# Moving the start addresses of the tiles that the matrix engine reads: a two-layer trunk in fp32r

## The chip, the cores and the metric

The kernel runs on one core of one Trainium2 chip. The time is device time in microseconds of that core, a median of several executions; one further execution was recorded by the hardware profiler, and every row of the profile below comes from it. Where a time in nanoseconds is given for "one matmul", the text says whether it is the duration of its record or the distance from its start to the start of the next one.

## The reference, cut to what matters

One sequence of 256 tokens with 2048 channels passes through two layers. Layer 0 mixes by a gated causal convolution beside a sparse attention of 16 heads, layer 1 by a causal pooling; each layer then has an MLP with a squared ReLU, 2048 to 8192 to 2048. All arithmetic is float32.

```
for layer in range(DEPTH):
    x = x + even_mixer(...) if layer % 2 == 0 else x + odd_mixer(...)
    x = x + mlp(x, mlp_norm[layer], w_mlp_in[layer], w_mlp_out[layer])
return rmsnorm(x, final_norm)

def mlp(x, g, w1, w2):
    h = rmsnorm(x, g) @ w1
    h = jnp.square(jax.nn.relu(h))
    return h @ w2
```

Nearly all the work is products of 256 tokens with weight matrices: the input and output projections of layer 0, and the two matrices of each MLP.

## The kernel before, in words

**Three products for one.** A float32 product is done as three products in the one-pass format fp32r. A weight unit of 128 partitions x 2048 floats is loaded into a tile `wraw`; ScalarE rounds it into `whi`, and VectorE writes the rest into `wlo` (class `Weights`, method `pieces`). The activations are split in the same way: `xT` holds, for each block of 128 channels, 256 columns of rounded values and 256 columns of rests. Then hi x hi, hi x rest and rest x hi are accumulated in PSUM. Every matmul goes through `mm` (line 194), so line 194 stands for all of them in the profile, and the names of the tiles tell them apart.

**Narrow and wide matmuls.** For a matmul the engine first loads 128 columns of one operand as its weights and then streams the other operand through. There are two shapes:

- narrow, in `unit_cols` (layer 0's projections) and in `unit_wide` and `first_hidden` (first matrix of the MLPs): 128 columns of `whi` or `wlo` are loaded, 256 columns of `xT` are streamed. In `keys_values` the roles are turned for the values: 128 columns of `xT` are loaded and 256 columns of `whi` or `wlo` streamed (shown as acc<-whi,xT).
- wide, in `product` (second matrix of the MLPs), in `by_token` (output projection, pooling) and in the end of `run_mlp`: 128 columns of an activation tile are loaded (the tiles `f11`, `f12`, `f22`, `s1` to `s4`, or `yo`, `yc`, `xT`) and 512 columns of `whi` or `wlo` are streamed.

In the profile the streamed operand and the loaded one stand behind the arrow (acc<-xT,whi is narrow, acc<-whi,f wide). Within a tile all these slices begin at multiples of 512 bytes from the tile's start, so each operand has the start of its tile, modulo 256 bytes, for all its matmuls.

**Order.** The program of each engine is written in order; the weight units come in the order of `_uses`, three raw tiles ahead (`RAW_BUFS`) and three split ones (`W_BUFS`). Between the products of the second matrix (12 wide matmuls each) stand units of the first matrix for the next chunk (48 narrow matmuls each).

**Where tiles lie.** A pool is a stretch of each partition, and its tiles follow one another in the order of their first use, each rounded up to 32 bytes. From the low end lie `const` (small tiles), `wpool` (three `wraw`, three `whi`, three `wlo`, 8192 bytes each) and `act` (the slot "xr", which holds `xraw`, `ctile` and the residual `x` in turn, then four slots of `xT`, 8192 bytes each, which `yo` and the residual's parts `xt` use too). A pool on the right side ends at the top of the partition, so a larger pool begins lower: `mix` in layer 0's mixer, `mlp` afterwards. Tiles named `fill` are never read or written; they only move what follows. Counted in bytes, the program before has these starts:

| tile | start | start modulo 256 |
|---|---|---|
| `wraw`, `whi`, `wlo` | 24640, 49216, 73792 (first of each three) | 64 |
| slot "xr" | 98368 | 64 |
| `xT`, `yo` | 115712 (first of four) | 0 |
| `kk2`, `klo` (keys, streamed) | 193024, 201216 | 0 |
| `yc`, `wg` | 155136, 163328 (the two slots that they share) | 0 |
| `q` (loaded for the scores) | 219008 | 128 |
| `f11` and the other forms | 193280 and on | 0 |
| `pm` (loaded for the pooling means) | 150176 | 160 |

Of the kernel before, what the change touches and what calls it, by code (L numbers as in the profile page):

```python
# [27 lines left out]
F32 = mybir.dt.float32  # L28
# [6 lines left out]
P = 128  # L35
# [6 lines left out]
HEADS = 16  # L42
# [137 lines left out]
def trunk(ctx: ExitStack, tc: tile.TileContext, a: dict, out: bass.AP, dump: dict | None = None):  # L180
# [3 lines left out]
    const = ctx.enter_context(tc.tile_pool(name="const", bufs=1, side="left"))  # L184
    wpool = ctx.enter_context(tc.tile_pool(name="wpool", bufs=1, side="left"))
    act = ctx.enter_context(tc.tile_pool(name="act", bufs=1, side="left"))
# [25 lines left out]
    nc.gpsimd.dma_start(ident, a["ident"])  # L212

    identr = const.tile([P, P], F32R, name="identr")
    const.tile([P, 32], F32, name="fill")
    neg_half = const.tile([P, 2], F32, name="neg_half")
    vector.memset(neg_half, -0.5)

# [59 lines left out]
    with ExitStack() as mx:  # L278
        mix = mx.enter_context(tc.tile_pool(name="mix", bufs=1, side="right", reuse_waits="tile"))
# [3 lines left out]
        def acc1(n=256, dt=F32):  # L283
            return ps.tile([P, 512], dt, tag="acc", bufs=8, name="acc")[:, 0:n]
# [86 lines left out]
        def unit_cols(*accs, done=lambda: None):  # L371

            ws = [W.next(16) for _ in accs]
            for u in range(4):
                X = xT[u]
                for acc, w in zip(accs, ws):
                    for k in range(4):
                        kk_ = 4 * u + k
                        st, sp = kk_ == 0, kk_ == 15
                        if len(w) == 1:  # L380
                            mm(acc, w[0][:, kk_], x32[kk_ // 8][:, kk_ % 8], start=st, stop=sp)
                        else:
                            hi, lo = w
                            mm(acc, hi[:, kk_], X[:, k, 0:256], start=st, stop=False)
                            mm(acc, hi[:, kk_], X[:, k, 256:512], start=False, stop=False)
                            mm(acc, lo[:, kk_], X[:, k, 0:256], start=False, stop=sp)
                if u == 3:
                    done()
                beside(u)
# [33 lines left out]
        def glu(g, late_g, a, late_a, out):  # L423
            sg = mix.tile([P, 256], F32, tag="row", bufs=4, name="sg")
            if late_g:
                vector.tensor_mul(sg, g, rbc)
            nc.scalar.activation(sg, sg if late_g else g, AF.Sigmoid)
            if late_a:
                vector.tensor_mul(sg, sg, rbc)
            vector.tensor_mul(out, a, sg)  # L430
# [4 lines left out]
        for ct in range(1, 8):  # L435
            g, a_ = acc1(), acc1()
            late = [W.used + i < PLAIN for i in range(2)]
            unit_cols(g)
            if ct == 1:

                ctile = act.tile([P, 8 * 286 + 8 * 256], F32, tag="xr", bufs=1, name="ctile")
                cin = ctile[:, 0:8 * 286].rearrange("p (c t) -> p c t", c=8)
                cacc = ctile[:, 8 * 286:].rearrange("p (c t) -> p c t", c=8)
                nc.gpsimd.memset(cin[:, :, 0:30], 0.0)
                glu(g0, True, a0, True, cin[:, 0, 30:286])
            unit_cols(a_)
            glu(g, late[0], a_, late[1], cin[:, ct, 30:286])
            conv_ready = ct + 1
# [4 lines left out]
        for i in range(2):  # L453
            t = mix.tile([P, KT, P], F32, tag="q8", bufs=2, name="w1")
# [5 lines left out]
        for i in range(2):  # L460
            t = mix.tile([P, 512], F32, tag="tt", bufs=3, name="wgl")[:, 0:384]
# [117 lines left out]
        keys_values(1)  # L579
        assert not steps  # L580

        gates = mix.tile([P, 2, HEADS, 3], F32, name="gates")
        pg = acc1()[0:112]
        for k in range(KT):
            X, w = xT[k // 4], wg[0][:, k]
# [7 lines left out]
        def gates_1():  # L593
# [5 lines left out]
            vector.tensor_add(g, g, pgt[:, :, 0:48])  # L599
            nc.scalar.activation(g, g, AF.Sigmoid)  # L600

        masks = const.tile([P, P + 33], F32, name="masks")
        nc.gpsimd.dma_start(masks, a["masks"])
        cmaskr = const.tile([P, P], F32R, name="cmaskr")
# [383 lines left out]

        banks_for("ps3")

        mix.tile([P, 24], F32, name="fill")
        x = act.tile([P, 2, D], F32, tag="xr", bufs=1, name="x")
        turns = []

# [21 lines left out]
    mlp = ctx.enter_context(tc.tile_pool(name="mlp", bufs=1, side="right", reuse_waits="tile"))  # L1016
# [240 lines left out]


    pm = mlp.tile([P, 3, 4, P], F32R, name="pm")

    def load_pm(i):
        pmf = mlp.tile([P, 4, P], F32, tag="s", bufs=3, name="pmf")
        nc.scalar.dma_start(pmf.rearrange("p g t -> p (g t)"), a["pm"][:, i * 512:(i + 1) * 512])
        return lambda: nc.scalar.activation(pm[:, i], pmf, AF.Copy)
# [233 lines left out]
```

## Time and profile before

| | |
|---|---|
| median of 3 runs | 1753.16 us (1749.74 to 1760.92) |
| the profiled execution: its own time | 1751.68 us |
| its span, first to last instruction | 1749.9 us |
| TensorE busy | 1737.2 us (99%), 11726 matmuls |
| VectorE busy | 1488.3 us (85%) |
| ScalarE busy | 1083.4 us (62%) |
| mean DMA rate | 229 GB/s |
| granted TensorE clock | 0.998 |

A record of a matmul lasts longer than the distance to the next one, because matmuls are pipelined: a row with 11726 matmuls of some 280 to 390 ns each adds up to less than their product. The rate at which the engine really goes is read from a stretch of time: its length divided by the number of matmuls that began in it. The answers by stretches count the records that lie in a stretch even in part; of the narrow and wide records two that began earlier still run at its start, so two are taken off the count.

### The profile page before, as it was taken

To read this page: it belongs to the slowest core of one execution; us is meant where nothing else is said; L and a number is where in the kernel's file an instruction comes from. 1 tells how busy PE (TensorE), PEld (TensorE's weight loads), DVE (VectorE), ACT (ScalarE), POOL (GpSimd) and SP (SyncE) were. 2 spreads that over 40 slices of the span, in tenths; PEclk is the share of its full clock that TensorE was granted. 3 is DMA by queue.
4 is the path that set the end of the run, shared out by engine and by line. 5 is a ranking of instruction groups with operands and counts; after the bars stand their busy time and mean duration, and the time that the engine had idled before them with its cause. 6 is when DMAs were issued, how large, how long until landed. Compare 5 with 4: busy or idle time off the path is not lost.

```text
span 1749.9 us, 28680 instructions
## 1 busy us (share of the span) xinstructions
PE 1737.2 (99%) x11726; PEld 1593.1 (91%) x11726; DVE 1488.3 (85%) x1851; ACT 1083.4 (62%) x1626; POOL 61.8 (4%) x82
## 2 busy tenths in 40 slices
PE   9999999999999999999999999999999999999997
PEld 7999998889999999999999989999999999999986
DVE  6998998766888888898889869688888889898985
ACT  4445666556666666665666655766665666666663
POOL 2000000000000000000000000000000000000000
PEclk9999999999999999999999999999999999999999
DMA  7654323546878787878778764687877787878873
GB/s 279 232 207 145 122 94 125 207 177 217 261 252 267 240 255 242 282 245 290 241 241 256 228 232 147 228 269 248 256 246 257 243 290 244 268 240 251 257 232 127
DMA packets 58948, 399.89 MB, mean 229 GB/s; under 512 B 6672, under 2 KB 7456, under 8 KB 11712
## 3 DMA queue, kind: packets, MB, share of 16 engines
q1 hardware_dynamic: 47904, 331.90, 49.3%
q0 software_dynamic: 8608, 61.49, 18.8%
q10 hardware_dynamic: 2304, 4.67, 0.8%
q8 instruction: 92, 1.51, 0.3%
q14 instruction: 40, 0.33, 0.1%
HBM read 395.93 MB, written 2.10 MB: 227 GB/s over the span
## 4 chain that ended last, share of the span: by engine, by line
PE 99%; issue 0%; DMA 0%; DVE 0%; ACT 0%; POOLq 0%; POOL 0%; ACTq 0%; DVEq 0%
PE acc L194 94%; PE S L194 2%; PE PV L194 1%; PE T L234 1%; PE acc L234 1%; PE T L194 0%; DMA xraw<-in_xT 0%; DVE x L78 0%; POOLq L1494 0%; POOL rs L1374 0%; DVE q L78 0%; ACT sq L1369 0%; DVE nb L78 0%; DVE wlo L78 0%; ACT yo L237 0%
## 5 line engine op out<-in xcount | busy, mean ns | idle before, releaser
L194 PE MATMUL acc<-xT,whi 128*128 128x256 f32 x4992 | 867.8, 278 | 0.0
L194 PEld LDWEIGHTS acc<-xT,whi 128*128 128x128 f32 x4992 | 763.6, 188 | 10.0
L78 DVE TENSOR_TENSOR wlo<-wraw,whi 128x1024 fp32r<-128x1024 f32 (+1 forms) x552 | 605.0, 1125 | 146.3 <-ACT whi L147 145.3
L194 PE MATMUL acc<-xT,wlo 128*128 128x256 f32 x2496 | 691.7, 277 | 0.0
L147 ACT ACTIVATE whi<-wraw 128x1024 fp32r<-128x1024 f32 (+1 forms) x552 | 515.3, 974 | 100.8 <-PE acc L194 85.0
L194 PEld LDWEIGHTS acc<-xT,wlo 128*128 128x128 f32 x2496 | 469.0, 188 | 0.0
L78 DVE TENSOR_TENSOR wlo<-z,whi 128x1024 fp32r<-128x1024 f32 x224 | 266.7, 1217 | 60.7 <-ACT whi L147 59.8
L194 PE MATMUL acc<-whi,s 128*128 128x512 f32 x960 | 315.9, 391 | 0.0
L147 ACT ACTIVATE whi<-z 128x1024 fp32r<-128x1024 f32 x224 | 230.5, 1054 | 93.9 <-DVE z L78 76.1
L194 PE MATMUL acc<-whi,f 128*128 128x512 f32 x864 | 282.3, 392 | 0.0
L194 PEld LDWEIGHTS acc<-whi,s 128*128 128x128 f32 x960 | 180.3, 188 | 35.8
L1045 ACT ACTIVATE t<-acc 128x256 f32<-128x256 f32 x128 | 48.8, 381 | 243.3 <-PE acc L194 242.8
L194 PEld LDWEIGHTS acc<-whi,f 128*128 128x128 f32 x864 | 162.3, 188 | 31.8
L194 PE MATMUL acc<-wlo,s 128*128 128x512 f32 x480 | 188.1, 392 | 0.0
L194 PE MATMUL acc<-wlo,f 128*128 128x512 f32 x432 | 169.3, 392 | 0.0
L194 PEld LDWEIGHTS acc<-wlo,s 128*128 128x128 f32 x480 | 90.1, 188 | 18.6
L78 DVE SCALAR_TENSOR_TENSOR ctile<-ctile,cw 128x256 f32<-128x256 f32 x240 | 102.1, 480 | 0.1
L194 PEld LDWEIGHTS acc<-wlo,f 128*128 128x128 f32 x432 | 81.1, 188 | 16.3
L78 DVE SCALAR_TENSOR_TENSOR x<-acc,r,x 128x512 f32<-128x512 f32 x110 | 81.2, 744 | 7.8 <-PE acc L194 7.8
L1090 ACT ACTIVATE s<-s 128x512 fp32r<-128x512 f32 x56 | 35.4, 632 | 62.5 <-DVE s L78 62.5
L78 DVE TENSOR_TENSOR z<-z,b 128x1024 f32<-128x1024 f32 x56 | 65.9, 1218 | 0.0
L78 DVE TENSOR_TENSOR z<-z,wraw 128x1024 f32<-128x1024 f32 x56 | 65.8, 1214 | 0.0
(213 smaller groups left out, 1360.3 us busy)
## 6 DMA issues: line engine op xcount, KB each, us to landing
wraw<-in_ws SPq DMA_DIRECT2D x254, 1024.0 KB, 6.4
z<-in_ws SPq DMA_DIRECT2D x28, 1024.0 KB, 7.2
b<-in_ws SPq DMA_DIRECT2D x28, 1024.0 KB, 4.8
b<-in_ws POOLq DMA_DIRECT2D x28, 1024.0 KB, 8.9
z<-in_ws POOLq DMA_DIRECT2D x28, 1024.0 KB, 8.3
w<-in_cmp_w POOLq DMA_DIRECT2D x2, 1024.0 KB, 6.8
xraw<-in_xT SPq DMA_DIRECT2D x3, 512.0 KB, 6.1
wraw<-in_ws SPq DMA_DIRECT2D x6, 256.0 KB, 6.2
```

Of the source, the lines that this page charges most:

```text
L78: return fn(*args, **kw)
L147: nc.scalar.activation(hi[:, c], raw[:, c], AF.Copy)
L194: nc.tensor.matmul(out, w, x, **kw)
L234: nc.tensor.transpose(out, src, ident[0:n, 0:n])
L1045: nc.scalar.activation(out, acc, AF.Relu)
L1090: nc.scalar.activation(F[tag][:, :, 0:P], src(), AF.Copy)
```

## The change

Only sizes and fillers change; no instruction is added, removed or moved.

```diff
@@ trunk, pool const @@
     identr = const.tile([P, P], F32R, name="identr")
-    const.tile([P, 32], F32, name="fill")
+    const.tile([P, 8], F32, name="fill")
@@ slot "xr" of pool act @@
-                ctile = act.tile([P, 8 * 286 + 8 * 256], F32, tag="xr", bufs=1, name="ctile")
+                ctile = act.tile([P, 8 * 286 + 8 * 256], F32, tag="xr", bufs=1, name="ctile",
+                                 padded_shape=[P, 8 * 286 + 8 * 256 + 32])
                 cin = ctile[:, 0:8 * 286].rearrange("p (c t) -> p c t", c=8)
-                cacc = ctile[:, 8 * 286:].rearrange("p (c t) -> p c t", c=8)
+                cacc = ctile[:, 8 * 286:8 * 286 + 8 * 256].rearrange("p (c t) -> p c t", c=8)
@@ pool mix @@
-        gates = mix.tile([P, 2, HEADS, 3], F32, name="gates")
+        gates = mix.tile([P, 128], F32, name="gates")[:, 0:96].rearrange("p (t h b) -> p t h b", t=2, h=HEADS)
@@ pool const @@
+        const.tile([P, 8], F32, name="fill2")
         masks = const.tile([P, P + 33], F32, name="masks")
@@ pool mix @@
-        mix.tile([P, 24], F32, name="fill")
+        mix.tile([P, 56], F32, name="fill")
@@ pool mlp @@
     pm = mlp.tile([P, 3, 4, P], F32R, name="pm")
+    mlp.tile([P, 40], F32, name="fill2")
```

What it does to the starts, worked out from the sizes: `const` loses 96 bytes at the first filler and gains 32 at the second, so `wpool` begins 64 bytes lower, at 24576, and all its tiles at multiples of 256. The slot "xr" then begins at 98304 and grows by 128 bytes (17344 to 17472), so `xT` begins at 98304 + 17472 = 115776, which is 64 beyond a multiple of 256. `mix` grows by 128 bytes at `gates` and 128 at its filler and begins 256 lower; the tiles after `gates` (`q` among them) go down by 128 and start at multiples of 256. `mlp` grows by 160 bytes behind `pm`, so `pm` begins 160 lower, at 150016, a multiple of 256, and everything behind it stays. Seen from the streamed operand, modulo 256, the loaded one lies:

| matmuls | streamed, loaded before | loaded from streamed | streamed, loaded after | loaded from streamed |
|---|---|---|---|---|
| narrow (xT, whi or wlo) | 0, 64 | 64 | 64, 0 | 192 |
| values (whi or wlo, xT) | 64, 0 | 192 | 0, 64 | 64 |
| wide with `f11`..., `s1`..., `yc` | 64, 0 | 192 | 0, 0 | 0 |
| wide with `yo`, `xT` | 64, 0 | 192 | 0, 64 | 64 |
| pooling means (forms, `pm`) | 0, 160 | 160 | 0, 0 | 0 |

## The prediction

> **What bounds the kernel now.** I read the shares by engine first, then the chain that ended last, then what TensorE waited for, and last the groups of instructions.
>
> ```profile
> PE 1737.2 (99%) x11726; PEld 1593.1 (91%) x11726; DVE 1488.3 (85%) x1851; ACT 1083.4 (62%) x1626; POOL 61.8 (4%) x82
> PE 99%; issue 0%; DMA 0%; DVE 0%; ACT 0%; POOLq 0%; POOL 0%; ACTq 0%; DVEq 0%
> PE acc L194 <- DVE zeros L78: 1.6, 1, 1.6
> PE acc L194 <- ACT x L312: 1.1, 1, 1.1
> L194 PE MATMUL acc<-xT,whi 128*128 128x256 f32 x4992 | 867.8, 278 | 0.0
> L194 PE MATMUL acc<-xT,wlo 128*128 128x256 f32 x2496 | 691.7, 277 | 0.0
> L194 PE MATMUL acc<-whi,s 128*128 128x512 f32 x960 | 315.9, 391 | 0.0
> L194 PE MATMUL acc<-whi,f 128*128 128x512 f32 x864 | 282.3, 392 | 0.0
> L194 PE MATMUL acc<-wlo,s 128*128 128x512 f32 x480 | 188.1, 392 | 0.0
> L194 PE MATMUL acc<-wlo,f 128*128 128x512 f32 x432 | 169.3, 392 | 0.0
> ```
>
> TensorE is busy for 99% of the span, the whole chain runs through it, and its longest waits are 1.6 and 1.1 us. Nothing else is late, so the time is the sum of the distances between matmul starts, and a change of addresses can matter only by changing those distances. There are 4992 + 2496 = 7488 narrow matmuls. The four wide groups shown are 2736; with 20 calls of `by_token` (16 in the output projection, 4 in the pooling) of 24 matmuls each, whose loaded tile is `yo`, `yc` or `xT`, I count 3216.
>
> **The distance differs between stages that do the same thing.** Stretches of TensorE alone, with columns time, busy time, count, granted clock, DMA share and rate; then the records of the tile `xT` in the first and in the third stretch, with shortest, median and longest duration:
>
> ```profile
> 40.00:120.00 80.00, 80.00 (x682) 1.00 0.63 233
> 168.60:179.90 11.30, 11.30 (x98) 1.00 0.50 178
> 394.00:422.00 28.00, 28.00 (x249) 1.00 0.59 226
> 426.16:431.63 5.47, 5.47 (x50) 1.00 0.92 235
> 431.63:437.12 5.49, 5.49 (x26) 1.00 0.87 278
> L194 PE MATMUL acc<-xT,whi x455: 281/281/281, 39.8 to 120.0; 128*128 128x256 f32 x152
> L194 PE MATMUL acc<-xT,whi x166: 276/276/276, 393.8 to 421.8; 128*128 128x256 f32 x166
> ```
>
> Two records that began earlier come off each count. From 40 to 120 us (`unit_cols`, narrow) a matmul starts every 80.00/680 = 117.6 ns. From 394 to 422 us (`first_hidden` and `unit_wide`, narrow, the same tiles at the same starts) it is 28.00/247 = 113.4 ns. The clock is 1.00 in both, and the durations don't scatter at all: 281 ns throughout one, 276 throughout the other. So there are a slow and a fast gait for one and the same pair of addresses, 4.2 ns apart. A unit of the MLP (426.16 to 431.63, 48 matmuls) is 5.47/48 = 114.0 ns, mostly fast. Two wide products (431.63 to 437.12, 24 matmuls) are 5.49/24 = 228.8 ns.
>
> How a unit of the MLP begins, row by row (start, time, records):
>
> ```profile
> 437.12 0.40 PE L194 MATMUL acc<-xT,whi 128*128 128x256 f32 x2
> 437.35 0.28 PE L194 MATMUL acc<-xT,wlo 128*128 128x256 f32 x1
> 437.47 0.40 PE L194 MATMUL acc<-xT,whi 128*128 128x256 f32 x2
> 437.71 0.28 PE L194 MATMUL acc<-xT,wlo 128*128 128x256 f32 x1
> 437.83 0.39 PE L194 MATMUL acc<-xT,whi 128*128 128x256 f32 x2
> 438.05 0.28 PE L194 MATMUL acc<-xT,wlo 128*128 128x256 f32 x1
> 438.17 0.39 PE L194 MATMUL acc<-xT,whi 128*128 128x256 f32 x2
> ```
>
> Three matmuls take 0.35, then 0.36 us, and from 437.83 on 0.34: it comes out of the wide products in the slow gait, and slips into the fast one after five matmuls. Which gait holds is thus decided by how a stretch is entered as well as by addresses.
>
> **What could be won.** A stream without any loss can be seen in the four first units, which are plain float32: nine records of 256 columns, each streamed at half the rate.
>
> ```profile
> 23.10 2.11 PE L194 MATMUL acc<-x,wraw 128*128 128x256 f32 x9
> L194 PE MATMUL acc<-x,wraw 128*128 128x256 f32 x128 | 28.6, 381 | 1.1 <-ACT x L312 1.1
> ```
>
> (2.11 - 0.38)/8 = 0.216 us for what 512 columns at full rate would take, against 228.8 ns for a wide fp32r matmul. An estimate of all that is lost: wide 3216 x 12.8 ns = 41 us; narrow, with 108 ns as half of 216, 7488 x 6.4 ns (from 114.4, the mean of both gaits by the counts given below) = 48 us. So 89 us, 5%, is the outer bound of any gain by addresses.
>
> A rule beside it: the Trainium skill, TensorE: Matmul & The Clock Gate, section "Back-to-back issue gap", gives N/2.4 + 2.5 ns for an isolated matmul, so 109.2 and 215.8 ns here; the trace has 113.4 to 117.6 and 228.8, and by that rule the outer bound would be some 81 us instead of 89.
>
> **The narrow matmuls after the change** stream from 64 beyond a multiple of 256 and load from 0, the loaded operand 192 from the streamed one. The trace has that very pair: the values in `keys_values`, with the roles turned, stream `whi` (64) and load `xT` (0).
>
> ```profile
> L194 PE MATMUL acc<-whi,xT x128: 276/279/383, 141.9 to 179.8; 128*128 128x256 f32 x128
> L194 PE MATMUL acc<-wlo,xT x64: 276/279/283, 142.1 to 179.7; 128*128 128x256 f32 x64
> L194 PE MATMUL acc<-xT,whi 128*128 128x256 f32 x536 | 94.9, 281 | 0.0
> L194 PE MATMUL acc<-xT,wlo 128*128 128x256 f32 x268 | 75.3, 281 | 0.0
> L194 PE MATMUL acc<-xT,whi x360: 276/281/469, 130.8 to 269.7; 128*128 128x256 f32 x180
> L194 PE MATMUL acc<-xT,wlo x181: 276/281/286, 129.8 to 269.8; 128*128 128x256 f32 x181
> ```
>
> In the stretch 168.60 to 179.90 above, the values start every 11.30/96 = 117.7 ns: the slow gait. Their shortest records are of 276 ns, so the fast gait occurs with this pair too. There is no third gait, and no loss-free one. So I take the narrow matmuls at nothing.
>
> The ends are all fast, or all slow. Slow now are the 804 up to 130 us (the two rows with 281), by the median rather more than half of the 541 between 130 and 271 us (I take 350), five in each of the 112 MLP units that follow wide products (560), and some 150 of the 192 values: 1860 x 4.2 ns = -8 us if all become fast. The other 7488 - 804 - 350 - 560 = 5774, if all become slow: +24 us.
>
> **The wide matmuls after the change** stream from a multiple of 256 (before: 64 beyond) and load from 0 (`f`, `s`, `yc`) or 64 (`yo`, `xT`). The trace has no such pair. The nearest rows with a stream from 0 are the scores' rests, loaded from 128 (the next load, `identr`, from 224), and the pooling means, loaded from 160:
>
> ```profile
> L194 PE MATMUL S<-klo,q 128*128 128x512 f32 x16 | 6.2, 390 | 0.0
> L194 PE MATMUL acc<-s,pm 128*128 128x512 f32 x20 | 5.3, 397 | 0.0
> L194 PE MATMUL acc<-f,pm 128*128 128x512 f32 x4 | 1.3, 396 | 0.0
> ```
>
> A record runs some 163 ns beyond the next start (391 against 228.8), so its duration tells the distance up to a constant. Streams from 0 last 390 and 397, those from 64 391 to 392: -1.5 to +5.5 ns, times 3216, is -5 to +18 us. With both operands at 0 there are only the gates, narrow and with 112 and 64 loaded columns in turn:
>
> ```profile
> 180.00:183.40 3.40, 3.40 (x31) 1.00 0.35 106
> ```
>
> 3.40/29 = 117.2 ns, which is no gain either. I take the row with many keys, klo, as the nearest (512 columns in one run, no odd start of 32 bytes as `pm` has): **-5 us**. The pooling means move from 397 to the wide's own value: 24 matmuls, 0.1 us. `q` (32 + 32 loads) is as small. What hides the rest, VectorE at 85%, needs no cover, because no instruction of it changes; DMA into `wraw` from 64 to 0 is the same number of bytes in the same order, and TensorE never waited for it.
>
> **The sum.** Execution profiled: 1751.7 us (span 1749.9 and 1.8 around it); 1751.7 + 0 (narrow) - 5 (wide) = 1746.7. The median of the runs lies 1.5 us higher, so the forecast is **1748 us**, no change as far as a measurement tells: about 1% (17.5 us) is what can be told from none here.
>
> **The rivals.**
>
> *The loss goes away* (chance 0.36). Both gaits show that some 5 to 9 ns per narrow and 13 ns per wide matmul are lost, and the streams differ only in where they read; a wide stream that starts at a multiple of 256 may lose less, and wide products then leave the narrow units in the fast gait at once. For it: the loss exists, it is as regular as a fixed conflict, and 512 columns lose more than twice what the fast 256 lose. Against: klo and the gates. Price: wide from 228.8 to twice the fast gait, 226.8, and all narrow fast: -6 - 8 = -14 us, 1739; half of the outer bound: -20 - 24 = -44 us, 1709. Its middle is 1724; it exceeds 1% where wide matmuls lose 3 ns less and narrow ones are fast.
>
> *The slow gait holds* (chance 0.22, the other side). Place: units of the MLPs, `unit_wide`. They slip out of the slow gait only after five matmuls; the values, with the new pair, stayed slow for the 96 matmuls from 168.6 to 179.9. If 4200 or more of the 5774 fast ones turn slow, the kernel is over 1% slower; all of them give +24, 1777, and with wide matmuls as slow as `pm`'s +18 more, 1795.
>
> *Addresses don't matter at all* (0.12, within the 0.42 of no change): 1753. For it: two gaits with the same addresses. Against: the gaits' unscattered durations, which look like a fixed pattern of reads. The Trainium skill, SBUF — State Buffer, section "Who interferes with whom", says that TensorE has two independent read ports and never waits on anyone; by that rule the start of one operand against the other is free and the time stays at 1753. The trace agrees in that nothing shows a conflict directly, but 113.4 and 117.6 ns for the same work are not explained by it. No run here shows the addresses alone.
>
> **How the numbers follow.** No change 0.42 (forecast 0.30, no effect 0.12; 1736 to 1770), faster by over 1% 0.36, slower by over 1% 0.22. The range takes in the larger part of the first rival and all narrow matmuls slow: 1713 to 1778. About 0.08 of the faster side (more than half of the loss gone) and 0.08 of the slower (slow and `pm`-like) are left out.
>
> **What the changed profile would show.** By the forecast: TensorE still 99%; records of 276 ns in the MLP's narrow units and of 281 from 40 to 120 us; wide ones at 390. Rival one: wide records below 389 or narrow ones below 276. Rival two: medians of 281 after 394 us. If a third gait appears, my use of the values as the model of the new pair is wrong.

## The result, and the profile after

The changed kernel takes 1775.57 us (median of 6 runs, 1774.57 to 1776.43) against 1752.15 us of the kernel before in the same comparison: 1.0122 times as long, 95% interval 1.0093 to 1.015. It is slower by 23 us in the median (21 us by the ratio): the interval is clear of no change, and its middle, though not its lower end, lies beyond 1%. The profiled execution has a span of 1772.8 us against 1749.9.

Shares by engine, chain and TensorE's waits of the kernel after:

```profile
PE 1760.5 (99%) x11726; PEld 1617.1 (91%) x11726; DVE 1490.1 (84%) x1851; ACT 1084.6 (61%) x1626; POOL 61.8 (3%) x82
PE 98%; DVE 1%; issue 0%; DMA 0%; ACT 0%; POOLq 0%; POOL 0%; ACTq 0%; DVEq 0%
PE acc L194 <- DVE zeros L78: 1.6, 1, 1.6
PE acc L194 <- ACT x L312: 0.8, 1, 0.8
```

As before, TensorE is the bound, with the same number of matmuls and no new wait. It is busy for 23.3 us more, which is all of the loss. So every microsecond lies in the distances between matmul starts. The records of `xT` (shortest, median, longest) in one layer's MLP before; then three stretches after (time, busy time, count, clock, DMA share, rate), the same records of `xT`, and two of the wide groups:

```profile
L194 PE MATMUL acc<-xT,whi x1718: 276/276/285, 449.8 to 995.7; 128*128 128x256 f32 x191
```

```profile
40.00:120.00 80.00, 80.00 (x682) 1.00 0.63 233
439.10:444.76 5.66, 5.66 (x50) 1.00 0.80 292
444.76:450.23 5.47, 5.47 (x26) 1.00 0.92 216
L194 PE MATMUL acc<-xT,whi x1696: 279/280/283, 450.2 to 999.2; 128*128 128x256 f32 x189
L194 PE MATMUL acc<-whi,s 128*128 128x512 f32 x960 | 315.9, 391 | 0.0
L194 PE MATMUL acc<-wlo,s 128*128 128x512 f32 x480 | 186.6, 389 | 0.0
```

The first fence is the kernel before, the second the kernel after. The early stretch hasn't moved: 682 records in 80 us, 117.6 ns each, slow as before. A narrow unit of the MLP takes 5.66 us instead of 5.47 (48 matmuls, 117.9 ns instead of 114.0), and its shortest record is now 279 ns: the fast gait, whose records were 276, is gone from the MLP. Two wide products take 5.47 us instead of 5.49; the wide records last 391 ns with `whi`, as before, and 389 instead of 392 with `wlo`.

Summed over the whole trace, from each matmul's start to the next one's: the 7488 narrow matmuls with `xT` streamed and the 32 of the gates take 889.2 us instead of 864.2 (+25.0), the wide ones 737.2 instead of 738.6 (-1.4), all others 135.1 instead of 135.7 (-0.6). The sum is +23.0, as the spans differ by 22.9.

A unit begins thus in the kernel after (timeline rows; those of before stand in the prediction):

```profile
439.10 0.40 PE L194 MATMUL acc<-xT,whi 128*128 128x256 f32 x2
439.34 0.28 PE L194 MATMUL acc<-xT,wlo 128*128 128x256 f32 x1
439.46 0.40 PE L194 MATMUL acc<-xT,whi 128*128 128x256 f32 x2
439.69 0.28 PE L194 MATMUL acc<-xT,wlo 128*128 128x256 f32 x1
439.81 0.40 PE L194 MATMUL acc<-xT,whi 128*128 128x256 f32 x2
```

Three matmuls take 0.36, then 0.35, and it goes on so to the end of the unit. The slip into the fast gait after five matmuls doesn't come.

### The profile page after: what moved, and what is told of

It reads as the page before. It is cut to its first block, busy times and chain, and to the rows that moved or that the text cites. A ratio compares the mean times of both kernels' runs of the same rounds, so it can differ in the third digit from the quotient of the medians.

```text
span 1772.8 us, 28679 instructions
## 1 busy us (share of the span) xinstructions
PE 1760.5 (99%) x11726; PEld 1617.1 (91%) x11726; DVE 1490.1 (84%) x1851; ACT 1084.6 (61%) x1626; POOL 61.8 (3%) x82
## 4 chain that ended last, share of the span: by engine, by line
PE 98%; DVE 1%; issue 0%; DMA 0%; ACT 0%; POOLq 0%; POOL 0%; ACTq 0%; DVEq 0%
PE acc L194 94%; PE S L194 2%; PE PV L194 1%; PE T L234 1%; PE acc L234 1%; DMA xraw<-in_xT 0%; DVE wlo L78 0%; PE T L194 0%; DVE ctile L78 0%; DVE o_tok L78 0%; DVE x L78 0%; DVE yo L78 0%; POOLq L1497 0%; POOL rs L1377 0%; DVE q L78 0%
## 5 line engine op out<-in xcount | busy, mean ns | idle before, releaser
L194 PE MATMUL acc<-xT,whi 128*128 128x256 f32 x4992 | 892.0, 280 | 0.0
L78 DVE TENSOR_TENSOR wlo<-b,whi 128x1024 fp32r<-128x1024 f32 x56 | 65.9, 1221 | 0.0
```

Of the source, the lines that this page charges most:

```text
L78: return fn(*args, **kw)
L194: nc.tensor.matmul(out, w, x, **kw)
```

## The experiments

Three theories to begin with. **A**: the distance of the loaded operand from the streamed one, modulo 256 bytes, fixes the gait of the narrow matmuls. **B**: the wide matmuls' addresses do it, by the way in which they hand over to the narrow ones. **C**: what counts is that the streamed operand begins at a multiple of 256. "Distance" is always the start of the loaded operand less that of the streamed one, modulo 256. All runs but e15 start from the changed kernel and set some of its fillers otherwise; "wide distance" is that of the MLP's wide matmuls. The ns are start to start, from the traces: narrow over the 112 MLP units of 48 matmuls that follow wide products, wide inside the MLP's products.

| run | xT, weights, forms start at | narrow distance | wide distance | narrow ns | wide ns | us | ratio to before (95%) |
|---|---|---|---|---|---|---|---|
| before | 0, 64, 0 | 64 | 192 | 113.9 | 228.8 | 1751 to 1752 | |
| after | 64, 0, 0 | 192 | 0 | 117.8 | 228.5 | 1775.57 | 1.0122 (1.0093 to 1.015) |
| e1 | 192, 0, 0 | 64 | 0 | 117.8 | 226.7 | 1766.77 | 1.0096 (1.0081 to 1.0111) |
| e2 | 0, 0, 0 | 0 | 0 | 119.8 | 228.0 | 1787.79 | 1.0214 (1.0199 to 1.023) |
| e3 | 128, 0, 0 | 128 | 0 | 119.9 | 228.9 | 1790.29 | 1.023 (1.0213 to 1.0247) |
| e4 | 0, 64, 0 | 64 | 192 | 113.9 | 228.8 | 1748.5 | 0.9995 (0.9986 to 1.0004) |
| e5 | 0, 64, 64 | 64 | 0 | 117.8 | 226.7 | 1765.2 | 1.0073 (1.0058 to 1.0088) |
| e6 | 64, 0, 192 | 192 | 192 | 117.8 | 229.3 | 1777.42 | 1.0144 (1.0127 to 1.0161) |
| e7 | 192, 0, 192 | 64 | 192 | 113.9 | 228.9 | 1750.31 | 0.9995 (0.998 to 1.0011) |
| e8 | 192, 0, 64 | 64 | 64 | 115.8 | 233.1 | 1772.95 | 1.0118 (1.0103 to 1.0133) |
| e11 | 192, 0, 128 | 64 | 128 | 114.6 | 232.2 | 1766.66 | 1.0089 (1.0074 to 1.0104) |
| e12 | 160, 0, 192 | 96 | 192 | 118.6 | 228.7 | 1783.3 | 1.0185 (1.0168 to 1.0202) |

### The start of xT alone: e1, e2, e3

```diff
-                                 padded_shape=[P, 8 * 286 + 8 * 256 + 32])
+                                 padded_shape=[P, 8 * 286 + 8 * 256 + 0])    # e1; + 16 in e2, + 48 in e3
```

> Only the start of xT moves against the changed kernel, from 64 to 192 beyond a multiple of 256 (the slot before it is not padded); whi and wlo stay at 0, the forms at 0. The loaded operand of the narrow matmuls then lies 64 from the streamed one, as before the change, with other starts. Theory A (the distance of the two starts, modulo 256, decides the gait of the narrow matmuls): the MLP's narrow records are back at a median of 276 ns, TensorE some 25 us shorter than the changed kernel, about 1750 us. Theory B (the wide matmuls, now at 0 and 0, hand over in a phase that keeps the narrow ones slow): 281 ns and about 1775 us. Theory C (what counts is that the streamed xT begins at a multiple of 256): still slow, about 1775 us.

> Only the start of xT moves against the changed kernel, from 64 to 0 (16 floats of padding in the slot before it instead of 32); whi, wlo and the forms stay at 0, so both operands of every large matmul begin at multiples of 256. Theory A (distance): a distance of 0 is untried; the gates' 117.2 ns in the profile before speak for the slow gait, about 1775 us. Theory B (the hand-over from the wide matmuls): 281 ns, about 1775 us. Theory C (the start of the streamed operand): 276 ns in the MLP, about 1750 us.

> Only the start of xT moves against the changed kernel, from 64 to 128 (48 floats of padding), the distance of the loaded operand becomes 128. Theory A gives either gait, and the four distances 0, 64, 128 and 192 then have one each; theory B 281 ns and 1775 us; theory C 281 ns and 1775 us.

Records of `xT` in the MLP of layer 0 and in the early stretch in e1; the same records of the MLP and the early stretch's count in e2; the records of the MLP in e3:

```profile
L194 PE MATMUL acc<-xT,whi x1699: 281/281/281, 449.7 to 1000.0; 128*128 128x256 f32 x189
L194 PE MATMUL acc<-xT,whi x468: 276/276/280, 39.9 to 119.8; 128*128 128x256 f32 x156
```

```profile
L194 PE MATMUL acc<-xT,whi x1664: 277/283/283, 453.3 to 995.7; 128*128 128x256 f32 x185
40.00:120.00 80.00, 80.00 (x669) 1.00 0.63 232
```

```profile
L194 PE MATMUL acc<-xT,whi x1664: 279/282/284, 452.9 to 996.3; 128*128 128x256 f32 x185
```

Theory C falls: with xT at a multiple of 256, e2 is among the slowest. Theory A alone falls too: e1 has the distance of before, and its narrow matmuls run fast from 40 to 120 us (276 ns) and slow in every MLP unit (281). So one pair of starts has both gaits in one execution. The distance sets which gaits there are: with 128 columns loaded, 0 and 128 show none below 118 ns in a long stretch (in e2 80.00/667 = 119.9 ns at each matmul), while 64 and 192 show 113.3 and 117.8.

### The large operands put back: e4

```diff
-    const.tile([P, 8], F32, name="fill")
+    const.tile([P, 24], F32, name="fill")
...
-                                 padded_shape=[P, 8 * 286 + 8 * 256 + 32])
+                                 padded_shape=[P, 8 * 286 + 8 * 256 + 0])
```

> The large operands as before the change (whi and wlo at 64, xT at 0), by a first filler of 24 floats and no padding behind ctile; the rest of the change stays (gates, q, pm, the fillers of mix and mlp). If the large operands alone carry the loss: 276 ns in the MLP's narrow records, wide ones at 391 to 392, 1752 us within 0.3%. If q, pm or the constants carry it: up to 1775 us.

```profile
L194 PE MATMUL acc<-xT,whi x1724: 276/276/285, 449.9 to 996.9; 128*128 128x256 f32 x192
```

1748.5 us, 0.9995 times before: `q`, `pm`, the gates and the constants cost nothing that shows. The loss lies in the starts of the weights and of xT.

### The wide distance alone: e5, and both back by other starts: e6, e7, e8

```diff
 # e5: weights at 64, xT at 0 (as e4), and the forms 64 bytes up by a smaller filler at the end of pool mlp
-    mlp.tile([P, 56], F32, name="fill")
+    mlp.tile([P, 40], F32, name="fill")       # e8 too; 72 floats in e6 and e7 (forms at 192)
-    mlp.tile([P, 40], F32, name="fill2")
+    mlp.tile([P, 56], F32, name="fill2")      # keeps pm at 0; 88 floats in e6 and e7
```

> whi, wlo at 64 and xT at 0 as before the change, but the forms of the MLP (loaded by the wide matmuls) begin at 64 instead of 0, so that the wide matmuls' loaded operand lies 0 from the streamed one, as in the changed kernel, while the narrow ones keep the addresses of before. Theory B (the wide matmuls' own gait decides in which gait the narrow ones that follow them run): wide ones at 226.7 ns and the MLP's narrow ones at 117.8 without a slip, 1767 to 1776 us. Theory A (the distance of the narrow operands alone): 113.8 ns as before, about 1745 to 1750 us.

> The changed kernel with one thing more: the forms begin at 192 instead of 0, so that the wide matmuls' loaded operand lies 192 from the streamed one, as before the change, while the narrow ones keep the changed addresses. Theory B: wide ones back at 226, 229 and 232 ns in turn, the MLP's narrow ones fast after some five matmuls, about 1752 us. Theory A (narrow distance 192 is bad in itself): the narrow ones stay at 117.8 ns, 1775 us.

> xT at 192 (narrow distance 64 as before the change, whose stretch from 35 to 130 us ran at 113.4 ns with these starts) and the forms at 192 (wide distance 192 as before). Theory B: MLP narrow ones fast after a slip as before the change, wide ones at 229, and the early stretch fast: some 4 us below before, 1747 us. Theory A without a hand-over: the MLP stays as in the run with xT at 192 and the forms at 0, 1767 us.

> As the last, but the forms at 64, so that the wide distance is 64, which no MLP product has had. Theory B: the gait of the wide matmuls is open (226.7 or 229 ns) and with it that of the narrow ones: 1747 us if they are fast, 1767 if slow. Theory A: as the run with xT at 192 and the forms at 0, 1767 us.

One MLP unit, two wide products and the records in e5; a unit and the records in e6; the records and the early stretch of e7; and in e8 a unit, two wide products and the next unit:

```profile
447.80:453.45 5.65, 5.65 (x49) 1.00 0.51 122
442.36:447.80 5.44, 5.44 (x27) 1.00 0.97 215
L194 PE MATMUL acc<-xT,whi x1698: 281/281/281, 449.9 to 999.9; 128*128 128x256 f32 x189
```

```profile
440.61:446.27 5.66, 5.66 (x50) 1.00 0.84 321
L194 PE MATMUL acc<-xT,whi x1686: 277/280/283, 451.8 to 999.9; 128*128 128x256 f32 x188
```

```profile
L194 PE MATMUL acc<-xT,whi x1728: 275/276/286, 450.1 to 997.7; 128*128 128x256 f32 x192
40.00:120.00 80.00, 80.00 (x682) 1.00 0.63 231
```

```profile
435.97:441.63 5.66, 5.66 (x50) 1.00 0.89 343
441.63:447.23 5.60, 5.60 (x27) 1.00 0.89 168
447.23:452.69 5.46, 5.46 (x50) 1.00 0.46 131
```

e5 gives the narrow matmuls exactly what they had before and changes only what the wide ones load. Its wide matmuls get faster (24 in 5.44 us, 226.7 ns) and the narrow ones that follow them get slow (5.65 us a unit): +0.7%, which is theory B. Its narrow stretch from 394 to 422 us, ahead of the MLP's first wide product, stays at 113.3 ns, as before. But e6, with the changed narrow addresses and the wide distance of before, is as slow as the changed kernel, against theory B alone. e7 has both distances of before with other starts, and the time of before. So within these runs the distances count and not the starts (e1 and e5, alike in both distances with other starts, are 0.2% apart and have the same gait in all 112 units), and the change spoilt the fast gait twice: the wide distance of 0 with a narrow one of 64 is slow, the narrow distance of 192 with a wide one of 192 is slow, and the change has both. e8 adds that a wide distance of 64 costs 4.3 ns per wide matmul against 192, and that its units are fast or slow in a fixed order, 56 of each (5.66 and 5.46 us above; 115.8 ns in the mean): the same starts in the same execution, entered after different products.

The early stretches of e1 and e7 have the same instructions and the same starts, and ran at 113.4 ns in the one (276 ns records) and 117.6 in the other (682 in 80 us), so what was expected of e7, a fast early stretch and 1747 us, did not come. Some 800 matmuls in the other gait are worth 3 to 4 us. What picks the gait there is not shown: each kernel has one trace, and the spread of e7's executions (1748.36 to 1753.64 us) would fit a choice that differs from execution to execution.

e7 shows one thing more. Its values in `keys_values` stream `whi` from 0 and load `xT` from 192: the distance of 192 that the same values had in the kernel before, where they were slow (117.7 ns) and where the changed kernel's narrow matmuls are slow. Here they are fast, with no instruction added:

```profile
L194 PE MATMUL acc<-whi,xT x64: 275/276/278, 169.7 to 180.4; 128*128 128x256 f32 x64
```

### Entering the units another way: e9, e10, e13 to e16

One small matmul ahead of each of the 120 calls of `unit_wide` shifts the instant at which the unit begins, and changes no address. Its output is overwritten by the first real matmul. It also puts another load and another stream just ahead of the unit, so these runs vary the entry as a whole; whether the instant alone decides they don't tell.

```diff
         hi, lo = W.next(16)
+        mm(acc[:, 0:32], hi[:, 0], xT[0][:, 0, 0:32], start=True, stop=True)                # e9, e10, e15: 128 columns loaded
+        mm(acc[0:32, 0:32], hi[:, 0, 0:32], xT[0][:, 0, 0:32], start=True, stop=True, ...)   # e13, e14: 32 loaded
+        mm(acc[0:32, 0:128], hi[:, 0, 0:32], xT[0][:, 0, 0:128], start=True, stop=True, ...) # e16: 32 loaded, 128 streamed
```

> The run with xT at 192 (narrow distance 64, wide distance 0, MLP narrow ones slow at 117.8 ns) with one matmul more at the head of each unit_wide: 32 columns of xT into the accumulator, which the first real matmul overwrites; 120 of them, some 112 ns each (kcT's small matmuls before), +13 us. Theory B (the instant at which the wide matmuls hand over decides): the narrow ones enter at another instant, the fast gait becomes possible, 113.4 ns and 1767 + 13 - 25 = 1755 us. If the wide matmuls set the gait in some lasting way, not by the instant: 117.8 ns, 1780 us.

> The changed kernel (narrow distance 192, wide distance 0) with the same 32-column matmul ahead of each unit_wide. If distance 192 is slow however it is entered: 117.8 ns, 1775 + 13 = 1788 us. If only the instant of entry matters: some units fast, down to 1763 us.

> Narrow distance 64, wide distance 0 (xT at 192, forms at 0; slow without an extra matmul, 1767 us, and slow with the 128-column-load one). Ahead of each unit_wide one matmul that loads 32 columns and streams 32: some 30 to 60 ns, +4 to 7 us. Theory B (the instant of entry alone): another instant, so either gait; if fast, 1767 + 5 - 25 = 1747 us, below the kernel before. If distance 64 after wide ones at distance 0 is slow at any instant: 1772 us.

> The changed kernel with the same short matmul ahead of each unit_wide. Theory B: either gait by the instant; fast 1775 + 5 - 25 = 1755 us, slow 1780 us.

> The kernel before (narrow distance 64, wide distance 192, MLP units fast after five matmuls) with the matmul of 128 loaded and 32 streamed columns that made the changed kernel fast. Theory B (the instant of entry): either gait, 1752 + 11 = 1763 us if fast, 1785 if the new instant is one of the slow ones. If distance 64 prefers the fast gait after wide ones at 192: 1763 us.

> Narrow distance 64, wide distance 0 with a matmul of 32 loaded and 128 streamed columns ahead of each unit_wide, some 55 to 110 ns, +7 to 13 us: a third instant of entry at this distance. Theory B: either gait, 1752 us if fast, 1777 if slow. Three slow entries out of three would speak for a preference of this pair of distances.

Records of `wlo` in the MLP, free of the small matmul, in e10 (the changed kernel with it), e14 (the changed kernel with the shorter one), e9 and e16 (narrow distance 64, wide distance 0):

```profile
L194 PE MATMUL acc<-xT,wlo x857: 276/276/276, 451.0 to 999.7; 128*128 128x256 f32 x172
```

```profile
L194 PE MATMUL acc<-xT,wlo x832: 278/279/281, 453.1 to 995.9; 128*128 128x256 f32 x167
```

```profile
L194 PE MATMUL acc<-xT,wlo x837: 281/281/281, 449.9 to 999.7; 128*128 128x256 f32 x168
```

```profile
L194 PE MATMUL acc<-xT,wlo x855: 275/276/287, 449.8 to 998.2; 128*128 128x256 f32 x171
```

| run | narrow, wide distance | small matmul, loaded x streamed | gait of the 112 units after wide products | us | ratio to before (95%) |
|---|---|---|---|---|---|
| e10 | 192, 0 | 128 x 32 | fast from the first | 1762.92 | 1.0072 (1.0057 to 1.0087) |
| e14 | 192, 0 | 32 x 32 | slow | 1786.94 | 1.0178 (1.0136 to 1.022) |
| e9 | 64, 0 | 128 x 32 | slow | 1782.41 | 1.0183 (1.0166 to 1.02) |
| e13 | 64, 0 | 32 x 32 | fast after four | 1757.94 | 1.0027 (1.0005 to 1.005) |
| e16 | 64, 0 | 32 x 128 | fast after four | 1758.48 | 1.0021 (0.9997 to 1.0045) |
| e15 | 64, 192 (before) | 128 x 32 | fast after four | 1765.3 | 1.0062 (1.0038 to 1.0086) |

e10 is the plainest answer: the changed kernel with its addresses untouched and 120 matmuls *more* is 12.7 us faster (1762.92 against 1775.57, with the kernel before at 1751.46 and 1752.15 beside them), because its 112 units after wide products run at 113.3 ns. The other 8, which follow narrow matmuls in the first part of each MLP, have the same small matmul and the same starts and run at 117.8. The same two small matmuls act the other way round at the other distance (e14 and e9 slow, e10 and e13 fast). So at distances 64 and 192 alike both gaits are open to a unit, and with the starts given the entry decides. The small matmul costs what it may win: in e10 the two distances at the head of a unit are 28 and 201 ns instead of one of 114, some 13 us in all, so none of these kernels beats the one before.

### The other distances: e11, e12

```diff
-    mlp.tile([P, 56], F32, name="fill")        # e11: xT at 192 as e1, forms at 128
+    mlp.tile([P, 24], F32, name="fill")         # and fill2 of 72 floats, so that pm stays
-                                 padded_shape=[P, 8 * 286 + 8 * 256 + 32])    # e12: xT at 160, forms at 192 as e6
+                                 padded_shape=[P, 8 * 286 + 8 * 256 + 56])
```

> Narrow distance 64 as before the change, wide distance 128 (forms at 128), the last of the four multiples of 64 for the wide ones. The wide distances 0 and 192 gave 226.7 and 228.8 ns, 64 gave 233. Theory B: narrow ones fast or slow by the hand-over; by symmetry with the narrow ones, where 0 and 128 are alike, the wide ones at 128 run as at 0 and hand over as there: 117.8 ns, about 1767 us; else 1750 us.

> xT at 160, the narrow distance 96, not a multiple of 64, wide distance 192 as before the change. If only the 64-byte piece in which a row begins counts: like distance 64 or 128, that is 113.9 or 119.9 ns and 1750 or 1785 us. If the distance counts more finely: a gait of its own, below 113 ns at best (each ns is 7.5 us).

Two wide products of e11:

```profile
443.25:448.82 5.57, 5.57 (x26) 1.00 0.92 185
```

What was expected of e11 didn't come: the wide matmuls at distance 128 aren't as at 0 but 5.5 ns slower (5.57 us for 24, 232.2 ns over all products), and 84 of the 112 units after them are fast (114.6 in the mean). e12 shows a distance between two multiples of 64 to be no better: 118.6 ns.

## Why the prediction was wrong

**What held.** TensorE as the only bound; no work of another engine moved. The two gaits, their sizes (113.4 and 117.6 ns; 113.3 and 117.8 in the steady parts) and the outer size of a loss. The values of `keys_values` were a right model of the new pair: neither a third gait nor a loss-free one came, and even the slow records' length is theirs (medians of 279 and 280 ns, where the old pair's are 281). The small parts (`pm`, `q`) were nothing, as e4 shows.

**The step that failed** is "So I take the narrow matmuls at nothing". From the values I read, rightly, that both gaits exist for the new pair, and took the share of each to stay as well, though the same section had said that the gait "is thus decided by how a stretch is entered as well as by addresses", and though the change altered both. Its own upper end, all remaining 5774 narrow matmuls slow, was +24 us; the term measured +25.0 us instead of 0, and 21.4 of them lie in the 112 MLP units, of which none left the slow gait any more. The second rival, with its place (the MLP's units) and its price (1777 us), is what happened; its mark, medians of 281 ns after 394 us, came as 279 and 280, with no record below 279 from 450 to 1000 us. The measured 1775.57 us lies inside the range of 1713 to 1778 only because the range took that rival in. Its chance of 0.22 was too low. Its reason was half the truth: the new pair stayed slow for 96 matmuls in a row, but not because distance 192 is slow by itself (e10's units and e7's values run it fast).

**The wide term** was -5 us and came out at -1.4: -2.0 for the 2736 matmuls of the MLPs, -0.4 for those with `yc`, and +1.0 for the 288 that load `yo` or `xT`, whose distance became 64 and not 0. In the steady part of a product the MLP's wide matmuls did fall, to 226.7 ns, as e1 and e5 show throughout. But in the changed kernel the first seven of a product that follows a unit take 241, 224, 231, 236, 228, 232 and 231 ns (start to start), which gives most of the gain back. That isn't left over from the slow gait: e1 and e5 have no such head after slow units at distance 64, and e10 has one of five matmuls after fast units at distance 192. What makes it is open. The row of klo was no guide: with `q` now at 0, both operands at 0, its own records went from 390 to 396 ns, while the MLP's wide matmuls got faster at the same distance of 0:

```profile
L194 PE MATMUL S<-klo,q 128*128 128x512 f32 x16 | 6.3, 396 | 0.0
```

**The first rival** (the loss goes away) had its condition met in part, wide matmuls 2 ns better in the steady part, and failed on the narrow ones, which it had assumed would follow. At a narrow distance of 64 the wide distance of 0, which makes the wide ones better, is what makes them slow (e5); at the changed kernel's 192 they are slow with a wide distance of 192 too (e6). The stream without loss that priced it, 216 ns and 108 as its half, was an estimate from the plain float32 units: no steady stretch of a run came below 226.7 and 113.3 ns. **"Addresses don't matter at all"** is excluded by e7, e6 and e12, which differ in the start of xT alone (192, 64 and 160) and take 1750.31, 1777.42 and 1783.3 us. The Trainium skill, SBUF — State Buffer, section "Who interferes with whom", says that TensorE waits on no one; here, where the profile shows TensorE waiting for nothing and a clock of 1.00, the distance of its two operands and the entry set the time from one narrow matmul to the next, between 113.3 and 119.9 ns, and the measurement decides.

What stays open is what the gaits are made of. The runs show which distances have a fast gait and that the entry picks one; why they do, no run here tests.

## What to carry to other kernels

Where TensorE is busy all the time, read the distance between matmul starts by stage, and look at the spread of the records: two sharp values for the same operands are two steady states, and a change that touches neither work nor waits can move the kernel between them. A term that depends on such a state is not worth nothing because both states exist before and after; ask what each stage is entered from, and give the worse state its full chance. To test whether addresses or entry are to blame, change the entry without moving an address, as e10 does.

## What the runs showed of the hardware

- In these kernels fp32r matmuls with 128 loaded and 256 streamed columns start every 113.3 or 117.8 ns at distances of 64 and 192 bytes (modulo 256) from the streamed operand to the loaded one, 119.9 ns at 0 and 128 in the MLP, 118.6 at 96. With 512 streamed columns it is 226.7 ns at a distance of 0 once steady, 228.8 at 192, 232.2 at 128 and 233.1 at 64.
- With both distances kept, other starts changed nothing that shows: e7 against before, 0.9995 (0.998 to 1.0011).
- A gait, once settled, lasted up to 800 matmuls; in e10 one small matmul at the head switched all 48 of a unit, 4.5 ns each, in the 112 units that follow wide products, and in none of the 8 that follow narrow matmuls.
- The best distance for the wide matmuls (0) hands over badly to the narrow ones: e5 wins 6 us on the wide ones and loses 20 on the narrow ones against before.
